# A decoder block: gate outputs in their own pool, column pairs alternating, rotation steps written later

## The chip, the cores and the metric

The kernel runs on one core of a Trainium2 chip. The metric is the device time of one execution in microseconds. TensorE (PE) multiplies, VectorE (DVE), ScalarE (ACT) and GpSimd (POOL) do the elementwise work, and all DMAs are issued from SyncE's queue (SP). An engine executes its own instructions in the order in which they stand in its queue, and a framework that turns the traced program into these queues decides that order from its own estimate of when each instruction is ready, unless the program pins it.

## The reference

A block of a decoder on 1024 tokens of width 1024, in float32. What matters here is the first half:

```
h = rms_norm(x, ln1_g)
proj = h @ w_in + b_in
rq, rk, rv, rg, aq, ak, av, gate_a, gate_b = split(proj)
rq, rk = rotary(rq), rotary(rk)             # 4 heads of 128
ry = head_group_norm(retention(rq, rk, rv)) # 4 heads of 256
branch_a = (silu(rg) * ry) @ w_ret_out
ay = sliding_window_sink_attention(rotary(aq), rotary(ak), av)
branch_b = ay @ w_attn_out
merged = sigmoid(gate_a) * branch_a + sigmoid(gate_b) * branch_b
x = x + merged @ w_out
x = x + (silu(h2 @ w_gate) * (h2 @ w_up)) @ w_down   # h2 = rms_norm(x, ln2_g)
return rms_norm(x, lnf_g)
```

## The kernel before

Every float32 operand of a matmul is split in a high and a low half, and a product is the sum of three matmuls (high by high, high by low, low by high). A split is a ScalarE copy (the high half) and a VectorE subtraction (the low half), lines 125 to 127. Stages follow each other on one PE queue:

- **Attention** (from 272). The pool `w1` holds all its tiles. While 32 units of attention run, PE's free time is filled with the 16 gate columns (`gate`, 470 to 476): each gate column is two halves of 24 matmuls in a PSUM bank of the tag `acc`, a tanh on ScalarE into a tile of the tag `st` (473), and a write of that tile to the DRAM tensor `tb_d` (475). After the last attention unit, `fl.rest()` (513) finishes the gates that are left. Then `w1` closes.
- **Retention values** (562 to 687). The pool `rvp` opens where `w1` was; it holds `vacc`, an accumulator of 32 KB a partition, whose free parts are scratch space first. The product `h @ w_rv` is done by a scheme of seven half-size products (P1 to P7, in the place of eight), each of four steps of 12 matmuls (line 646). Before the first step VectorE makes sums and differences of quarters of `h` in `vacc` (lines 660 to 676, 13 additions and subtractions of 128 x 1024, by `vadd` and `vsub`, lines 577 and 580), with the splits of the first two weight blocks (`vprep`, which writes `vP`) behind them. VectorE and ScalarE are pinned to the written order here (`in_order`, 659; the helper is at 101).
- **Column pairs** (690 to 815). The eight pairs of 128 columns for retention's k, q and swish gate are computed by the same scheme: `wseq` (698) lists the 56 products, 12 matmuls each (770), pair by pair with neighbours interleaved. `cols` (559) lists the pairs: four for k and q, then four for the gate. At each product, `wprep_to` splits the operand of the product two ahead; with the first two blocks of a pair it issues four weight differences on POOL (`gsub`, 516). `wproduct` issues the matmuls, keeps partial results (`p1`, `u2`, `u3`, line 775), and hands each of the four finished 128 x 512 results of a pair to `wresult` (735). For a gate pair that is an addition (755), a Silu (757) and a write to `rg_d` (758). For a k or q pair it is an eviction with the bias (743 or 745) into a tile `r`, two DMAs that swap the halves of its partitions into `xw` (747, 748), a multiplication of `r` by the cosines on VectorE (749), one of `xw` by the sines on POOL (750), their sum on VectorE (751), and a write to `rk_d` (752). The tables of cosines and sines sit in the buffers `kT` and `qT` of the pool `kq` (693), which head 0's k and q take over afterwards (`load_kq`, 799). P3 of a pair adds to the PSUM bank (`wB`) that P5 left, and can begin only when the result that reads that bank has been evicted. The order of VectorE, ScalarE and POOL is left to the framework in this stage.
- **Retention** (818 on). The pool `w2` opens over the places of the two previous pools; `load_v` (839) and `load_g` (845) fetch what the heads need, `k_transpose` turns k, and the output columns of attention (`bb_g`, 829), which read `ay` (loaded by `load_ay`, 792), fill PE's time. The first of `w2`'s instructions wait for the release of the pools below.

Then come the merge, the output product and the FFN, on which the diff does not touch.

Of the kernel before, what the change touches and what calls it, by code (L numbers as in the profile page):

```python
# [10 lines left out]
F32 = mybir.dt.float32  # L11
# [3 lines left out]
ALU = mybir.AluOpType  # L15

P = 128
# [9 lines left out]
RH = 4  # L27
AH = 16
C_RQ, C_RK, C_RV, C_RG, C_AQ, C_AK, C_AV, C_GA, C_GB = (
    0, 512, 1024, 2048, 3072, 4096, 4224, 4352, 5376)  # L30


def f32(t):
    return t.bitcast(F32)
# [3 lines left out]
def hybrid_block(ctx: ExitStack, tc: tile.TileContext, x, ln1_g, w_in, b_in, ret_norm_g, w_ret_out,  # L38
                 attn_sinks, w_attn_out, w_out, ln2_g, w_gate, w_up, w_down, lnf_g,
                 c_ident, c_atab, c_rtab, c_amask, c_rmask, c_rcol, out):  # L40
    nc = tc.nc
    x = x[0]
    out = out[0]
# [18 lines left out]
    rk_d = dram.tile([8, P, S], F32, name="rk_d")  # L62
# [37 lines left out]
    @contextmanager  # L100
    def in_order(*engines):

        traced = nc.cur_bb.bb.instructions
        last = traced[-1]
        yield
        start = next(k for k in reversed(range(len(traced))) if traced[k] is last) + 1
        prev = {}
        for i in traced[start:]:
            if i.engine in engines:
                if i.engine in prev:  # L110
                    tc.add_manual_dep(i, prev[i.engine],
                                      mybir.DependencyInfo(mybir.DependencyClass.NoSync, mybir.DependencyReason.DATA),
                                      reason="in_order")
                prev[i.engine] = i.name
# [41 lines left out]
    def dense_g(src, col, X, evac, name):  # L156
        w = slab(src, col, name)
        for half in range(2):
            pt = acc(f"acc_{name}_{half}")
            yield from mm_g(pt, w, X, half * 512)  # L160
            evac(half, pt)
            yield
# [57 lines left out]
    for t in range(NB):  # L220
# [3 lines left out]
        if 1 <= t <= 2:  # L224
            raw = raw_slab([8, P], f"kv{t}")
            c = C_AK if t == 1 else C_AV
# [42 lines left out]
    nc.vector.tensor_scalar(out=nsink, in0=nsink, scalar1=-1.0, scalar2=None, op0=ALU.mult)  # L269


    with tc.tile_pool(name="w1", bufs=1) as w1:
        atab = w1.tile([P, 2, S], F32, name="atab")
        nc.sync.dma_start(atab, c_atab.rearrange("z p s -> p z s"))
        amask = w1.tile([P, 256], F32, name="amask")
# [4 lines left out]
        def r512(tag, bufs, name):  # L280
            return w1.tile([P, 512], F32, tag=tag, bufs=bufs, name=name)
# [188 lines left out]
        def gate(n):  # L470

            def evac(half, pt):
                t = r512("st", 2, f"tb{n}{half}")
                nc.scalar.activation(t, pt, AF.Tanh, bias=bhalf[:, n:n + 1], scale=0.5)
                nc.sync.dma_start(tb_d[n, :, half * 512:half * 512 + 512], t)
            return dense_g(w_in, C_GA + n * P, H, evac, f"g{n}")
# [11 lines left out]
        for i in range(NU + 1):  # L488
# [7 lines left out]
            if i > 0:  # L496
                u_values(i - 1)
                if i % 4 == 0:
                    g, b, _, Bt, jb, _ = geo(i - 1)
                    c = slice((b // 4) * 512, (b // 4) * 512 + 512)  # L500
# [7 lines left out]
            if i == 3 * NB:  # L508

                for k in range(4):  # L510
                    nc.gpsimd.tensor_tensor(out=wv[:, 4 + k, :], in0=wv[:, 12 + k, :], in1=wv[:, 4 + k, :],
                                            op=ALU.subtract)
# [43 lines left out]
    def kq_pair(name, shape):  # L556
        return [kq.tile([P] + shape, F32, tag=t, name=f"{name}{t}") for t in ("kT", "qT")]

    cols = [C_RK, C_RQ, C_RK + 256, C_RQ + 256] + [C_RG + 256 * h for h in range(RH)]
    NW = len(cols)  # L560

    with tc.tile_pool(name="rvp", bufs=1) as rvp:
# [96 lines left out]
        with in_order(nc.vector.engine, nc.scalar.engine):  # L659
# [18 lines left out]
            for n in range(28):  # L678
                pr, k = VORDER[n // 4], n % 4
# [13 lines left out]
    rtab = kq_pair("rtab", [S])  # L693
    for z in range(2):
# [3 lines left out]
    wseq = [(0, "P2"), (1, "P2"), (0, "P1"), (1, "P1"), (0, "P6"), (0, "P5"), (0, "P7"), (1, "P6"), (0, "P4"), (0, "P3"),  # L698
            (1, "P5"), (1, "P7"), (2, "P1"), (1, "P4"), (1, "P3"), (2, "P2")]
# [7 lines left out]
    def wprep_to(n):  # L707
        while wready[0] < min(n, len(wseq)):
            j, pr = wseq[wready[0]]
            r0, r1 = wraw[j]  # L710
            b11, b12, b21, b22 = r0[:, :, 0:P], r0[:, :, P:2 * P], r1[:, :, 0:P], r1[:, :, P:2 * P]
            b = {"P1": b11, "P5": b11, "P7": b12, "P2": b21, "P4": b21, "P3": b22}.get(pr)
            if b is None:
                b = wtms[j]
            o = ring.tile([P, 2, 4, P], F32R, tag=("wh", "wl")[wready[0] % 2], name=f"w{j}{pr}")
            split(b, o[:, 0], o[:, 1])
            wops[j, pr] = o
            wdone.add((j, pr))
            if pr in ("P1", "P2") and {(j, "P1"), (j, "P2")} <= wdone:

                wtms[j] = wp.tile([P, 4, P], F32, tag="tt", bufs=2, name=f"wt2_{j}")
                gsub(b11, b12, b11)
                gsub(wtms[j], b22, b11)
                gsub(b12, b22, b12)
                gsub(b21, b21, wtms[j])
            if pr == "P3" and j + 2 < NW:
                wload_pair(j + 2)
            wready[0] += 1

    wbank, wkeep = {}, {}  # L730

    def wtile(tag, bufs, name):
        return wp.tile([P, 512], F32, tag=tag, bufs=bufs, name=name)

    def wresult(j, half, y, pt, other):

        ct = cols[j] // P + y
        bias = bcol[:, ct:ct + 1]
        c = slice(half * 512, half * 512 + 512)
        r = wtile("r", 4, f"r{j}{half}{y}")  # L740
        if j < 4:
            if other is None:
                nc.scalar.activation(r, pt, AF.Identity, bias=bias, scale=1.0)
            else:
                nc.vector.scalar_tensor_tensor(out=r, in0=pt, scalar=bias, in1=other, op0=ALU.add, op1=ALU.add)
            xw = wtile("xw", 2, f"xw{j}{half}{y}")
            nc.sync.dma_start(xw[0:64, :], r[64:128, :])
            nc.sync.dma_start(xw[64:128, :], r[0:64, :])
            nc.vector.tensor_tensor(out=r, in0=r, in1=rtab[0][:, c], op=ALU.mult)
            nc.gpsimd.tensor_tensor(out=xw, in0=xw, in1=rtab[1][:, c], op=ALU.mult)  # L750
            nc.vector.tensor_tensor(out=r, in0=r, in1=xw, op=ALU.add)
            nc.sync.dma_start(rk_d[ct, :, c], r)
            return
        if other is not None:
            nc.vector.tensor_tensor(out=r, in0=pt, in1=other, op=ALU.add)
            pt = r
        nc.scalar.activation(r, pt, AF.Silu, bias=bias, scale=1.0)
        nc.sync.dma_start(rg_d[ct - C_RG // P, :, c], r)

    def wproduct(j, pr):  # L760
        kind = {"P1": "A", "P6": "A", "P7": "A", "P4": "A", "P2": "C", "P5": "B", "P3": "B"}[pr]
        first = pr in ("P1", "P2", "P5")
        if first:
            tag, bufs = {"A": ("acc", 3), "B": ("s", 2), "C": ("t", 2)}[kind]
            wbank[j, kind] = ps(tag, bufs, f"w{kind}{j}")
        pt = wbank[j, kind]
        o = wops.pop((j, pr))
        for k, (xh, xl) in enumerate(HX[pr]):
            for z, (w, v) in enumerate(((0, xh), (0, xl), (1, xh))):
                nc.tensor.matmul(pt, o[:, w, k, :], v, start=(first and k + z == 0), stop=(k == 3 and z == 2),  # L770
                                 skip_group_check=not first)

        def keep(tag, bufs):
            e = wtile(tag, bufs, f"{tag}{j}")
            nc.scalar.copy(e, pt)
            wkeep[j, tag] = e
        if pr == "P1":
            keep("p1", 2)
        elif pr == "P6":
            keep("u2", 2)  # L780
        elif pr == "P7":
            keep("u3", 1)
        elif pr == "P4":
            wresult(j, 1, 0, pt, None)
        elif pr == "P3":
            wresult(j, 0, 1, pt, wkeep.pop((j, "u2")))
        if pr in ("P5", "P7") and (j, "u3") in wkeep and (j, "B") in wbank:
            wresult(j, 1, 1, wbank[j, "B"], wkeep.pop((j, "u3")))
        if pr in ("P1", "P2") and (j, "p1") in wkeep and (j, "C") in wbank:
            wresult(j, 0, 0, wbank[j, "C"], wkeep.pop((j, "p1")))  # L790

    def load_ay(z):
        AY.append(act.tile([P, 8, 1024], F32R, tag="B", name=f"ay{z}"))
        for g in range(2):
            nc.sync.dma_start(f32(AY[z][:, 4 * g:4 * g + 4, :]), ay_d[2 * z + g])
# [3 lines left out]
    def load_kq(h, z):  # L799

        t = (kTs, qTs)[z][h] = kq.tile([P, S], F32, tag=("kT", "qT")[z], name=f"r{z}{h}")
        nc.sync.dma_start(t, rk_d[4 - 4 * z + h])

    for i, (j, pr) in enumerate(wseq):
        wprep_to(i + 3)
        wproduct(j, pr)
        if (j, pr) == (2, "P1"):
            load_ay(0)
        elif (j, pr) == (NW - 2, "P6"):
            load_kq(0, 0)  # L810
            load_kq(0, 1)
        elif (j, pr) == (NW - 1, "P7"):
            load_ay(1)
    wpp.__exit__(None, None, None)
    wsc.__exit__(None, None, None)

# [327 lines left out]
    for nh in range(2):  # L1144
# [20 lines left out]
        for t in range(NB):  # L1165
# [12 lines left out]
            if nh == 1:  # L1178
# [3 lines left out]
                r = rstd_of(m2, 1, f"ln2_{t}")  # L1182
# [249 lines left out]
    for pi, pr in enumerate(ORDER):  # L1432
# [23 lines left out]
        for tt in range(4):  # L1456
            for f in range(cut, NP):
                mms(f, tt)
            half, z = {"P1": (0, 0), "P5": (1, 1), "P6": (0, 1), "P2": (0, 0), "P7": (1, 1), "P4": (1, 0),
                       "P3": (0, 1)}[pr]  # L1460
            t = 4 * half + tt
# [67 lines left out]
```

## Time and profile before

| what | value |
|---|---|
| median of 3 runs | 1643.65 us (1643.48 to 1647.53) |
| the profiled execution's own time | 1642.58 us |
| its span, first to last instruction | 1640.8 us |
| TensorE busy | 1585.0 us, 97% |
| VectorE busy | 971.6 us, 59% |
| ScalarE busy | 713.7 us, 43% |
| GpSimd busy | 384.4 us, 23% |
| mean granted TensorE clock | 0.987 |
| column pairs, first to last matmul | 498.4 to 661.9 us |

All times in the trace count from the span's start. A name such as `vacc` or `r` stands for all tiles of that name with numbers left out, `vacc<-h` means that `vacc` is written from `h`, and L646 is line 646. In the view of waits a line "A <- B: total, times, longest" tells how long the engine of A stood idle before that instruction because B was not done. In a timeline, brackets give the idle time before an instruction and what ended it. PEclk is the share of full speed that TensorE's clock was granted. SPq is SyncE's queue, where DMAs are issued.

### The profile page before, as it was taken

The numbers are of one execution on the slowest core, as the hardware profiler recorded it, in microseconds if no ns is written. First come the engines' busy times: TensorE is split into PE (matmuls) and PEld (weight loads), VectorE is DVE, ScalarE is ACT, GpSimd is POOL, SyncE is SP. The second block draws the span as 40 slices with busy tenths as digits, with TensorE's granted clock in tenths as the row PEclk, the third lists the DMA queues.
The fourth block names the chain that finished last, engine by engine and source line by source line (L and its number), as shares of the span: only waits on it lengthen the run. The fifth ranks groups of instructions, "written<-read, shape, count | busy, mean of one in ns | idle before, by whom it ended". The sixth has DMA issues, their size and how long they took to land.

```text
span 1640.8 us, 20874 instructions
## 1 busy us (share of the span) xinstructions
PE 1585.0 (97%) x7507; PEld 1317.1 (80%) x7507; DVE 971.6 (59%) x1730; ACT 713.7 (43%) x1415; POOL 384.4 (23%) x321
## 2 busy tenths in 40 slices
PE   9999999998799899999999998999999999999998
PEld 8887888886688778878888886888888888788886
DVE  6468767662875673677655248544444444588756
ACT  5358777762223234454322145333333333344445
POOL 2000001000005551000000025655555666300001
PEclk9999999999899999999999999999999999999999
DMA  6554638223026452855454300333333333773323
GB/s 205 161 161 139 190 130 248 97 84 133 15 81 227 144 171 96 292 176 174 138 190 134 128 22 15 121 96 114 98 103 97 109 110 109 264 261 91 97 97 122
DMA packets 150869, 223.13 MB, mean 136 GB/s; under 512 B 9131, under 2 KB 83693, under 8 KB 149230
## 3 DMA queue, kind: packets, MB, share of 16 engines
q1 hardware_dynamic: 150766, 221.80, 41.6%
q8 instruction: 59, 0.97, 0.2%
q14 instruction: 44, 0.36, 0.1%
HBM read 149.67 MB, written 67.37 MB: 132 GB/s over the span
## 4 chain that ended last, share of the span: by engine, by line
PE 82%; DVE 8%; DMA 3%; ACT 3%; issue 2%; POOL 2%; SPq 0%; POOLq 0%; DVEq 0%; ACTq 0%
PE fA L1225 14%; PE fB L1225 7%; PE dA L1443 6%; PE dxP L1443 5%; PE wA L770 4%; PE acc_g L143 3%; PE acc_g L144 3%; PE acc_g L145 3%; PE fC L1225 3%; PE va L646 3%; PE vP L646 2%; PE acc_ba L145 2%; PE acc_ba L144 2%; PE acc_ba L143 2%; PE wo L1173 2%
## 5 line engine op out<-in xcount | busy, mean ns | idle before, releaser
L1443 PE MATMUL dA<-dwP,daP 128*128 128x512 f32 x528 | 121.4, 390 | 1.9 <-DVE dwP L127 1.9
L1443 PEld LDWEIGHTS dA<-dwP,daP 128*128 128x128 f32 x528 | 98.8, 188 | 23.8 <-DVE dwP L127 3.4
L143 PE MATMUL acc_g<-h,wh_g 128*128 128x512 f32 x256 | 100.3, 392 | 0.0
L144 PE MATMUL acc_g<-h,wh_g 128*128 128x512 f32 x256 | 100.2, 391 | 0.0
L145 PE MATMUL acc_g<-h,wl_g 128*128 128x512 f32 x256 | 99.9, 390 | 0.0
L1443 PE MATMUL dxP<-dwP,daP 128*128 128x512 f32 x396 | 90.2, 389 | 0.0
L1443 PEld LDWEIGHTS dxP<-dwP,daP 128*128 128x128 f32 x396 | 74.3, 188 | 15.4
L412 POOL COPY sc<-nsink 128x4 f32<-128x4 f32 x32 | 7.9, 249 | 308.5 <-PE pT L445 248.0
L1283 POOL TENSOR_TENSOR xf<-xf 128x512 f32<-128x512 f32 x44 | 70.0, 1592 | 35.9 <-issue 30.3
L427 ACT ACTIVATE sc<-sc,nm 128x257 f32<-128x257 f32 (+1 forms) x128 | 62.4, 491 | 26.3 <-DVE nm L424 26.0
L1236 POOL TENSOR_TENSOR xf<-xf 128x512 f32<-128x512 f32 x33 | 49.6, 1502 | 45.3 <-DVE xf L1241 26.7
L1246 ACT COPY xf<-fA 128x512 f32<-128x512 f32 x44 | 25.8, 588 | 75.8 <-PE fA L1225 75.8
L424 DVE CUSTOM_DVE_ANT_0 sc<-s,amask,nsink 128x256 f32<-128x256 f32 (+1 forms) x128 | 53.1, 460 | 9.4 <-PE s L421 9.0
L145 PEld LDWEIGHTS acc_g<-h,wl_g 128*128 128x128 f32 x256 | 48.1, 188 | 9.7
L143 PEld LDWEIGHTS acc_g<-h,wh_g 128*128 128x128 f32 x256 | 48.1, 188 | 9.2
L144 PEld LDWEIGHTS acc_g<-h,wh_g 128*128 128x128 f32 x256 | 48.1, 188 | 9.1
L127 DVE TENSOR_TENSOR dwP<-wd,dwP 128x512 fp32r<-128x512 f32 x77 | 54.7, 712 | 0.0
L1388 POOL TENSOR_TENSOR rs_f<-tot,mhalf 128x1 f32<-128x1 f32 x8 | 7.9, 992 | 197.9 <-DVE tot L1385 197.9
L516 POOL TENSOR_TENSOR wr_f<-wr_f 128x512 f32<-128x512 f32 x22 | 33.8, 1540 | 78.9 <-DVE t_4P L127 9.5
L143 PE MATMUL acc_bb<-ay,wh_bb 128*128 128x512 f32 x128 | 51.1, 401 | 0.0
L516 POOL TENSOR_TENSOR wr_wp<-wr_wp 128x512 f32<-128x512 f32 x8 | 11.5, 1436 | 167.6 <-DMA ay<-ay_d 148.0
L143 PE MATMUL aq<-h,wh_aq 128*128 128x512 f32 x128 | 50.1, 392 | 0.6 <-ACT wh_aq L362 0.6
(763 smaller groups left out, 4416.4 us busy)
## 6 DMA issues: line engine op xcount, KB each, us to landing
act_d<-xf SPq DMA_DIRECT2D x77, 256.0 KB, 2.1
daP<-act_d SPq DMA_DIRECT2D x21, 512.0 KB, 3.7
q_d<-stg SPq DMA_DIRECT2D x8, 1024.0 KB, 4.6
wr_g<-in_w_in SPq DMA_DIRECT2D x16, 512.0 KB, 5.2
q<-q_d SPq DMA_DIRECT2D x32, 256.0 KB, 6.2
tb_d<-tb SPq DMA_DIRECT2D x32, 256.0 KB, 2.1
ay_d<-q SPq DMA_DIRECT2D x8, 1024.0 KB, 6.1
ay<-ay_d SPq DMA_DIRECT2D x4, 2048.0 KB
```

The costliest lines, as they stand in the source:

```text
L127: nc.vector.tensor_tensor(out=lo, in0=raw, in1=f32(hi), op=ALU.subtract)
L143: nc.tensor.matmul(pt, hi[:, k, :], xh, start=(k == 0), stop=False)
L144: nc.tensor.matmul(pt, hi[:, k, :], xl, start=False, stop=False)
L145: nc.tensor.matmul(pt, lo[:, k, :], xh, start=False, stop=(k == 7))
L424: nc.vector.tensor_tensor_reduce(out=sc[:, j, 0:nk], in0=pt[:, jj * 256:jj * 256 + nk], in1=mk, scale=1.0, scalar=nsink[:, 4 * g + j:4 * g ...
L427: nc.scalar.activation(sc[:, j, 0:nk + 1], sc[:, j, 0:nk + 1], AF.Exp, scale=-1.0, bias=nm[:, j:j + 1], accum_out=den[:, j:j + 1])
L646: nc.tensor.matmul(vbanks[pr][tt], x_[:, c], w[:, u, :], start=(fresh and k + z == 0), stop=(k == 3 and z == 2), skip_group_check=not fresh)
L770: nc.tensor.matmul(pt, o[:, w, k, :], v, start=(first and k + z == 0), stop=(k == 3 and z == 2), skip_group_check=not first)
L1225: nc.tensor.matmul(pt, o[:, w, k, :], v, start=(first and k + z == 0), stop=(k == 3 and z == 2), skip_group_check=not first)
L1236: nc.gpsimd.tensor_tensor(out=dst[q], in0=dst[q], in1=sg[q], op=ALU.mult)
L1283: nc.gpsimd.tensor_tensor(out=o, in0=a, in1=b, op=op)
L1443: nc.tensor.matmul(banks[tt], a[:, u, c], w[:, v, :], start=(fresh and f + z == 0), stop=(f == NP - 1 and z == 2), skip_group_check=not fresh)
```

## The change

Three things change. The two gate tiles of the tag `st` move from `w1` to a pool `gt` of their own, which is allocated from the other side of SBUF, where the pool `kq` opens later. The list `cols` alternates: a k or q pair, a gate pair, and so on. And of a rotated result, only the eviction and the two swapping DMAs are issued at once; the two multiplications (`turn`) are written down two products later, the sum and the write to DRAM (`total`) three products later. For that `r` is split in two tags (`rr`, four buffers, for rotated results; `r`, two buffers, for gate results), `xw` has four buffers instead of two, and VectorE, ScalarE and POOL are pinned to the written order for the whole stage. The loads of head 0's k and q are written at the last pair's P5 instead of the seventh pair's P6.

```diff
-    with tc.tile_pool(name="w1", bufs=1) as w1:
+    with tc.tile_pool(name="gt", bufs=1, side="right") as gt, tc.tile_pool(name="w1", bufs=1) as w1:
...
-                t = r512("st", 2, f"tb{n}{half}")
+                t = gt.tile([P, 512], F32, tag="st", bufs=2, name=f"tb{n}{half}")
...
-    cols = [C_RK, C_RQ, C_RK + 256, C_RQ + 256] + [C_RG + 256 * h for h in range(RH)]
+    cols = [c for h in range(RH) for c in ((C_RK, C_RQ, C_RK + 256, C_RQ + 256)[h], C_RG + 256 * h)]
...
+    wlater, wnow = [], [0]
...
-        r = wtile("r", 4, f"r{j}{half}{y}")
-        if j < 4:
+        r = wtile(*(("r", 2) if j % 2 else ("rr", 4)), f"r{j}{half}{y}")
+        if j % 2 == 0:
...
-            xw = wtile("xw", 2, f"xw{j}{half}{y}")
+            xw = wtile("xw", 4, f"xw{j}{half}{y}")
             nc.sync.dma_start(xw[0:64, :], r[64:128, :])
             nc.sync.dma_start(xw[64:128, :], r[0:64, :])
-            nc.vector.tensor_tensor(out=r, in0=r, in1=rtab[0][:, c], op=ALU.mult)
-            nc.gpsimd.tensor_tensor(out=xw, in0=xw, in1=rtab[1][:, c], op=ALU.mult)
-            nc.vector.tensor_tensor(out=r, in0=r, in1=xw, op=ALU.add)
-            nc.sync.dma_start(rk_d[ct, :, c], r)
+
+            def turn():
+                nc.gpsimd.tensor_tensor(out=xw, in0=xw, in1=rtab[1][:, c], op=ALU.mult)
+                nc.vector.tensor_tensor(out=r, in0=r, in1=rtab[0][:, c], op=ALU.mult)
+
+            def total():
+                nc.vector.tensor_tensor(out=r, in0=r, in1=xw, op=ALU.add)
+                nc.sync.dma_start(rk_d[ct, :, c], r)
+            wlater.extend([(wnow[0] + 2, turn), (wnow[0] + 3, total)])
             return
...
-    for i, (j, pr) in enumerate(wseq):
-        wprep_to(i + 3)
-        wproduct(j, pr)
-        if (j, pr) == (2, "P1"):
-            load_ay(0)
-        elif (j, pr) == (NW - 2, "P6"):
-            load_kq(0, 0)
-            load_kq(0, 1)
-        elif (j, pr) == (NW - 1, "P7"):
-            load_ay(1)
+    with in_order(nc.vector.engine, nc.scalar.engine, nc.gpsimd.engine):
+        for i, (j, pr) in enumerate(wseq):
+            wprep_to(i + 3)
+            wnow[0] = i
+            wproduct(j, pr)
+            while wlater and wlater[0][0] <= i:
+                wlater.pop(0)[1]()
+            if (j, pr) == (2, "P1"):
+                load_ay(0)
+            elif (j, pr) == (NW - 1, "P5"):
+                load_kq(0, 0)
+                load_kq(0, 1)
+            if (j, pr) == (NW - 1, "P7"):
+                load_ay(1)
+        assert not wlater
```

## Prediction, made before the result was known

> **What bounds the kernel now.** I read the page first: spans, the busy shares, the chain that ended last.
>
> ```profile
> span 1640.8 us, 20874 instructions
> ...
> PE 1585.0 (97%) x7507; PEld 1317.1 (80%) x7507; DVE 971.6 (59%) x1730; ACT 713.7 (43%) x1415; POOL 384.4 (23%) x321
> ...
> PE 82%; DVE 8%; DMA 3%; ACT 3%; issue 2%; POOL 2%; SPq 0%; POOLq 0%; DVEq 0%; ACTq 0%
> ```
>
> TensorE (PE) bounds it. Its 56 us without a matmul are all that a change of waits can win, so the next question is in which stages they lie. The table of busy time by stage answers that (us, then busy time of each engine with its instructions, granted clock, DMA share, GB/s).
>
> ```profile
> core 0: us, PE busy (x) PEld busy (x) DVE busy (x) ACT busy (x) POOL busy (x), PEclk, DMA share, GB/s
> ...
> 400.70:433.10 32.40, 13.70 (x50) 10.62 (x49) 27.90 (x27) 5.51 (x8) 0.00 (x0) 0.68 0.18 57
> ...
> 498.40:529.00 30.60, 30.60 (x136) 25.34 (x136) 17.59 (x23) 10.37 (x18) 16.99 (x13) 1.00 0.68 227
> 529.00:605.00 76.00, 68.45 (x288) 54.52 (x288) 54.31 (x60) 23.10 (x39) 43.78 (x28) 0.98 0.49 146
> 605.00:661.90 56.90, 56.90 (x252) 46.73 (x252) 20.51 (x29) 26.66 (x43) 12.18 (x9) 1.00 0.42 144
> ```
>
> Two holes lie where the diff works: the start of the retention value product (400.7 to 433.1) and the rotated column pairs (529 to 605). The gate columns behind them (605 to 661.9) leave PE no hole. The chain gives each stage's ends and the pace of PE, and the waits name who is late.
>
> ```profile
> 401.86 1.99 DMA tb_d<-tb
> 404.33 2.37 DVE vacc L577 x2
> ...
> 420.70 12.40 PE va L646 x44
> 433.10 10.88 PE vP L646 x48
> ...
> 498.38 5.44 PE wC L770 x24
> ...
> 659.15 2.72 PE wB L770 x12
> ```
> ```profile
> DVE vacc L577 <- DMA tb_d<-tb: 23.1, 1, 23.1
> ...
> PE va L646 <- DVE vP L127: 18.3, 1, 18.3
> ```
>
> Twelve matmuls take 2.72 us where nothing is late (48 take 10.88). At 401.86 the last gate tile leaves for DRAM; only when it has landed does VectorE (DVE) begin its sums, and PE waits for the weight split that stands behind them.
>
> **The first hole: 21.1 us to win.** The value product is 28 steps of 12 matmuls, 28 x 2.72 = 76.2 us, and takes from 400.7 to 498.38, 97.7 us: 21.5 lost. What holds DVE is not the data:
>
> ```profile
> 375.76 0.43 DVE L468 TENSOR_TENSOR q<-tm,q 128x256 fp32r<-128x256 f32 x1 [0.47 <-ACT q L467]
> 379.96 1.23 DVE L127 TENSOR_TENSOR wl_g<-wr_g,wh_g 128x1024 fp32r<-128x1024 f32 x1 [3.77 <-ACT wh_g L126]
> ...
> 419.96 1.29 DVE L127 TENSOR_TENSOR vP<-wv,vP 128x512 fp32r<-128x512 f32 x2
> ```
> ```profile
> 401.89 0.50 PE L646 MATMUL va<-vP,h 128*128 128x512 f32 x1 [0.39 <-ACT tb L474]
> ```
>
> The sums read h, which has long been there; vacc lies in rvp, whose place was w1's. In the built program vacc (bytes 184064 to 216832 of a partition) does not touch the two gate buffers (225152 to 229248), and still waits for them: a new pool waits for all of the pool that it overlaps. With the gate tiles in gt, at the other side of SBUF, w1 is done with attention's last tiles, read at 375.76. DVE is then free from 381.2 (379.96 + 1.23). From 404.33 to the end of the first split at 420.6 it needs 16.3 us, so it would be ready at 397.5, 3.2 us ahead of the last gate matmul at 400.7. That gate work is the cover; without it the 16.3 come back. What is late next is a PSUM bank, which the last tanh frees: the 0.39 us in the last row stay, hence 21.1. kq now inherits gt's place and its wait for the landing at 403.9; its first tile is written after the second step of P1, past 406, so nobody waits. The third split needs a ring slot that the last gate gives back at its end, 400.7; its step comes two steps later, at 406.1.
>
> Of the 21.5, 2.4 are not waiting but slow matmuls: 44 should take 10.0 us and took 12.40, and the clock shows it.
>
> ```profile
> 420.66:425.00 4.34, 4.30 (x10) 3.43 (x11) 4.27 (x5) 0.48 (x1) 0.00 (x0) 0.50 0.02 4
> ```
>
> The granted clock is 0.50 for the first 4.3 us behind the wait, so removing the wait removes this as well. The Trainium skill (TensorE: Matmul & The Clock Gate, "What's actually happening") has an idle array at half clock until about 3.4 us of work release it, which would price this at 1.7 us as an estimate, and the first hole at 20.4; the 0.50 agrees, the length in this trace is longer.
>
> **The second hole: 11.2 us, of which I take 9.7.** 56 products x 2.72 = 152.3 us; from 498.38 to 661.87 they take 163.5, so 11.2 are lost. One rotated result, then the totals over the stage:
>
> ```profile
> 536.89 0.76 DVE r L745
> ...
> 538.23 4.31 DMA xw<-r
> ...
> 542.69 1.82 POOL xw L750
> ...
> 544.54 0.70 DVE r L751
> ```
> ```profile
> PEld wB L770 <- DVE r L745: 6.4, 3, 2.5
> ```
> ```profile
> DVE r L749 <- DMA xw<-r: 15.9, 9, 3.8
> ...
> DVE r L751 <- POOL xw L750: 11.1, 10, 2.4
> ```
>
> A result is evicted (536.89 + 0.76), its halves are swapped by two DMAs, GpSimd (POOL) multiplies, DVE adds. DVE works in order: its 27 us of waiting for the DMA and for POOL hold the next eviction, and P3 may not write bank B before that eviction has read it. The swap has landed 4.9 us after the eviction (537.65 to 542.54), POOL ends at 6.9. The change issues the multiplications two products later (5.44 us) and the add three later (8.16): 0.5 and 1.3 us to spare. The moved instructions are unchanged in number: per rotated result one POOL and two DVE operations, two swap DMAs and one write of rk_d; the swaps stay at the eviction, and the write goes down SP's queue behind the next result's swaps instead of ahead of them. Four xw and four rr buffers cover three products in flight. Alternation spreads the load: DVE's 92.4 us in the stage and POOL's 73.0 (three rows above) are 61% and 48% of 152.3, where now the rotated stretch has 71% and 58%. Pinning POOL puts a result's multiplication behind the four weight differences of the next pair, and DVE's add behind that. Not shown before; bounds: 0, as the gate columns lose, and 11.2, as now. I take 1.5, near the lower, because two products' slack (5.44) lies between an eviction and the matmul that needs its bank. A gain below 0 is excluded, PE being full there.
>
> The functions now alternate on ScalarE too (Identity, Silu). The trace has one load for it:
>
> ```profile
> 589.98 1.28 ACT L757 ACT_TABLE_LOAD   x1
> ```
>
> No second one appears when Identity returns at L945, so Silu's table serves both: one load, now at the first gate pair, with ScalarE at 30 to 47% busy (rows above): nothing. ScalarE is pinned as well: the copy for product i + 2 stands ahead of the eviction of product i, but its slot came free with product i - 2, so it holds nothing up.
>
> **The end of the stage: 1.5 us given back.** The last rotated pair is now last but one.
>
> ```profile
> 597.50 0.43 SPq L802 DMA_DIRECT2D r<-rk_d  x1
> ...
> 654.50 0.80 SPq L795 DMA_DIRECT2D ay<-ay_d  x2
> 658.98 4.73 SPq L758 DMA_DIRECT2D rg_d<-r  x3
> ...
> 670.98 0.59 SPq L843 DMA_DIRECT2D rv<-v_d  x1
> ```
> ```profile
> 679.32 0.36 PE L879 MATMUL u<-vh,kt 128*128 128x256 f32 x1 [0.25 <-issue]
> ```
> ```profile
> 660.00:670.00 10.00, 10.00 (x50) 8.38 (x49) 1.82 (x2) 1.54 (x2) 0.00 (x0) 1.00 1.00 364
> ```
> ```profile
> ACT kt L859 <- DMA rg_d<-r: 7.3, 1, 7.3
> ```
> ```profile
> DMA to landing us min/median/max: 7.1/7.1/7.1
> ```
>
> Loading head 0's k and q must wait for the cos and sin tables in the same buffers, now free four products (10.9 us, less POOL's 1.8) before the stage's end instead of 64.4 us before it. These 1.05 MB come close to the 4.2 MB of ay, in a stretch where the DMA engines are full: 0 to 2.9 us (1.05 MB at 364 GB/s). SP has them written behind ay, but it issues what its schedule finds ready (the present load, written at the seventh pair, went at 597.5), and the tables come free a little before P7 frees ay's place, which is three products or 8.2 us before the end. Gate results have two buffers instead of four: the last add must wait for the write issued at 658.98; at the last write's 7.1 us (last row) it lands at 666.1, against the add's 661.9: 0 to 4.2 us, in which DVE's split for the second output column waits too. All of w2 waits for the last landing, then come v's load and the matmul at 679.32, which has no slack. Bounds 0 and 7.1; I take 1.5, since fewer bytes are left to fetch by then.
>
> **Sum.** The profiled execution took 1642.58 us, 1.8 around its span and 1.07 below the median of 1643.65. 1642.6 - 21.1 - 11.2 + 1.5 + 1.5 = 1613.3; on the median's footing 1614.4.
>
> **Rivals.**
> (a) The first wait stays, because the release of gt still counts for rvp. For: vacc already waits without touching the tiles. Against: gt lies outside rvp. 1643.65 - 9.7 + 1.5 = 1635.5; chance 0.06.
> (b) The port that DVE and POOL share. A DVE operation of 0.70 us (the add above) took 1.77 while POOL subtracted:
>
> ```profile
> 555.99 1.77 DVE L749 TENSOR_TENSOR r<-r,rtabkT 128x512 f32<-128x512 f32 x1
> ```
> ```profile
> 555.48 1.74 POOL L516 TENSOR_TENSOR wr_wp<-wp,wr_wp 128x512 f32<-128x512 f32 x1
> ```
>
> Each turn now issues POOL's multiplication just ahead of DVE's own, so 16 x 1.07 = 17.1 us may be added to DVE. On PE's path in full it replaces the 11.2: 1643.65 - 21.1 - 11.2 + 17.1 + 1.5 = 1630.0; if it only keeps the hole as it is, 1624. Against: DVE's 39% idle. The Trainium skill (SBUF — State Buffer, "Who interferes with whom") says that the operation issued second fully blocks, which speaks against writing these two together; the 1.77 agrees. Chance 0.08.
> (c) The end of the stage costs its upper bound: 1614.4 + 5.6 = 1620. Chance 0.12.
> (d) Slower: the pinned DVE stands at every rotated result. If swaps land later than two products, say 7.0 us, the longest that POOL waited for one, each of 16 results costs 7.0 - 5.44 = 1.6 for the landing and 1.82 for POOL behind it: 54.7 us, 1643.65 - 32.3 + 54.7 = 1666. It turns the sign above 2.0 us per result. Against: 4.31 in a stretch of mean DMA share 0.49. Chance 0.02.
>
> ```profile
> POOL xw L750 <- DMA xw<-r: 29.0, 10, 7.0
> ```
>
> **Numbers.** The forecast has 0.72. The range, 1611 (nothing given back) to 1626, takes in (c) and the lower part of (b). About 0.3%, 4.9 us, is what a measurement of this kernel can tell from no change. Forecast, (a), (b) and (c) are faster by more: 0.96 with some left for mixtures; 0.02 within; 0.02 slower.
>
> **What would show it.** Right: DVE's first vacc sum at about 381, PE's first va step without a wait of over 1 us and a clock of 1.00 there; the 56 products in 152 to 155 us; PE waiting for L745 nowhere; xw's multiplication waiting under 1 us. Wrong: vacc waiting for tb_d, a clock below 1.00 in the column stage, PE idle at the first u by more than 3 us, or a stage that grew elsewhere.

## The result and the profile after

The changed kernel takes 1617.99 us (median of 4 runs, 1615.2 to 1620.9). Beside it on the same chip the kernel before took 1643.48 to 1647.53 us in three runs; a fourth took 4109.04 us and is left out of the ratio. The ratio is 0.9837 (95% interval 0.9808 to 0.9866). The profiled execution took 1616.76 us. Forecast were 1614.4 us, 1611 to 1626: faster, as said, and 3.6 us above the number.

The page of the changed kernel, the lines that answer to the first three of the prediction:

```profile
span 1615.0 us, 20843 instructions
...
PE 1579.4 (98%) x7507; PEld 1315.3 (81%) x7507; DVE 976.0 (60%) x1730; ACT 712.0 (44%) x1415; POOL 380.5 (24%) x321
...
PE 84%; DVE 6%; ACT 3%; DMA 3%; issue 2%; POOL 1%; SPq 0%; POOLq 0%; ACTq 0%; DVEq 0%
```

The span is 25.8 us shorter, DVE's share of the chain is down from 8 to 6%. To see where the time came from, one needs marks that both kernels have. Two are good: the first transposition of k (`kTT`), which PE reaches right behind the last of the 56 products, and the first matmul of the output product `acc_ba`, which ends the retention heads. Their instructions, kernel before and kernel after (the last two times are the first and the last start):

```profile
L770 PE MATMUL wC<-h,w0P x12: 389/389/389, 498.2 to 500.7; 128*128 128x512 f32 x12
L856 PE MATMUL kTT<-ident,r x32: 270/272/273, 661.7 to 765.0; 128*128 128x128 f32 x32
L143 PE MATMUL acc_ba<-yg,wh_ba x128: 389/389/477, 808.6 to 895.1; 128*128 128x512 f32 x128
```

```profile
L777 PE MATMUL wC<-h,w0P x12: 389/389/389, 477.3 to 479.8; 128*128 128x512 f32 x12
L868 PE MATMUL kTT<-ident,r x32: 270/272/273, 630.3 to 739.5; 128*128 128x128 f32 x32
L143 PE MATMUL acc_ba<-yg,wh_ba x128: 389/389/476, 783.4 to 869.9; 128*128 128x512 f32 x128
```

| stretch | before | after | difference | forecast |
|---|---|---|---|---|
| up to the first of the 56 products | 498.2 | 477.3 | -20.9 | -21.1 |
| the 56 products | 163.5 | 153.0 | -10.5 | -9.7 (-11.2 + 1.5) |
| from there to `acc_ba` | 146.9 | 153.1 | +6.2 | +1.5 |
| the rest | 832.2 | 831.6 | -0.6 | 0 |

The two holes closed as forecast. The third row is the miss: the heads behind the stage lose 6.2 us, not 1.5. First the holes. The chain of the changed kernel, with the start, the length and the work of each piece, and then the table of busy time by stage:

```profile
401.21 10.93 PE va L646 x48
412.14 10.88 PE vP L646 x48
...
466.55 10.88 PE va L646 x48
477.43 5.44 PE wC L777 x24
```

```profile
core 0: us, PE busy (x) PEld busy (x) DVE busy (x) ACT busy (x) POOL busy (x), PEclk, DMA share, GB/s
400.70:433.10 32.40, 32.40 (x145) 26.73 (x144) 24.12 (x31) 14.27 (x20) 0.00 (x0) 1.00 0.09 34
477.30:630.30 153.00, 152.84 (x673) 125.78 (x672) 95.75 (x111) 57.26 (x98) 68.66 (x48) 1.00 0.53 166
...
655.00:660.00 5.00, 4.53 (x26) 4.26 (x25) 3.77 (x12) 2.38 (x6) 0.00 (x0) 0.69 0.45 145
```

The value product now begins at once, 48 matmuls in 10.9 us, and the clock stays at 1.00 where it was 0.68 on average; in the 56 products PE is busy for 152.84 of 153.00 us. DVE had its sums done ahead of it, as its timeline shows:

```profile
376.15 0.43 DVE L468 TENSOR_TENSOR q<-tm,q 128x256 fp32r<-128x256 f32 x1 [0.47 <-ACT q L467]
376.66 2.36 DVE L577 TENSOR_TENSOR vacc<-h 128x1024 f32<-128x1024 f32 x2
...
393.31 1.28 DVE L127 TENSOR_TENSOR vP<-wv,vP 128x512 fp32r<-128x512 f32 x2
...
397.03 1.23 DVE L580 TENSOR_TENSOR vacc<-vacc 128x1024 f32<-128x1024 f32 x1
```

The first sum stands right behind attention's last tile; nothing waits for `tb_d`. Now the third row. SyncE's timeline, then DVE's, around the end of the 56 products, the waits there, and a line of ScalarE's timeline:

```profile
618.95 0.32 SPq L809 DMA_DIRECT2D r<-rk_d  x1
...
623.03 0.85 SPq L802 DMA_DIRECT2D ay<-ay_d  x2
628.12 0.90 SPq L765 DMA_DIRECT2D rg_d<-r  x2
629.07 6.66 SPq L132 DMA_DIRECT2D wr_bb<-in_w_attn_out  x2
640.18 0.34 SPq L765 DMA_DIRECT2D rg_d<-r  x1
...
643.48 0.45 SPq L853 DMA_DIRECT2D rmask<-in_c_rmask  x1
643.97 0.59 SPq L855 DMA_DIRECT2D rv<-v_d  x1
```

```profile
626.65 0.69 DVE L762 TENSOR_TENSOR r<-wB,u 128x512 f32<-128x512 f32 x1
638.71 0.69 DVE L762 TENSOR_TENSOR r<-wB,u 128x512 f32<-128x512 f32 x1 [11.37 <-DMA rg_d<-r]
641.67 1.23 DVE L127 TENSOR_TENSOR wl_bb<-wr_bb,wh_bb 128x1024 fp32r<-128x1024 f32 x1 [2.28 <-ACT wh_bb L126]
```

```profile
POOL xw L753 <- DMA xw<-r: 45.0, 12, 8.7
...
DVE r L762 <- DMA rg_d<-r: 11.4, 1, 11.4
...
PE u L891 <- issue: 3.6, 1, 3.6
```

```profile
652.85 1.34 ACT L912 ACTIVATE vh<-rv,rcol 128x512 fp32r<-128x512 f32 x2 [4.73 <-DMA rv<-v_d]
```

Read them in this order. The last gate addition stands still for 11.4 us, until 638.71, since of the two buffers neither is free: the write that would free one was issued at 628.12 and took 10.6 us. Its own result is written at 640.18 (at about 632 where it has not to wait, as in e3 below). The pool `w2` opens behind that write, and the mask's and v's loads go out at 643.5 and 644.0, 3.3 and 3.4 us later than in e3. The first `u` comes at 653.7, 23.4 us behind the first `kTT` (before: 679.3 - 661.7 = 17.6). The view of waits names nothing for which PE stands still there ("issue"), but `u` reads `vh`, and ScalarE makes `vh` only at 652.85, when v has landed. PE is idle for 3.6 us in front of `u`, and its granted clock is 0.69 from 655 to 660.

### The profile page after: what moved, and what is told of

Its sections match the earlier page's. It is cut to its first block, busy times and chain, and to the rows that moved or that the text cites. A ratio compares the mean times of both kernels' runs of the same rounds, so it can differ in the third digit from the quotient of the medians.

```text
span 1615.0 us, 20843 instructions
## 1 busy us (share of the span) xinstructions
PE 1579.4 (98%) x7507; PEld 1315.3 (81%) x7507; DVE 976.0 (60%) x1730; ACT 712.0 (44%) x1415; POOL 380.5 (24%) x321
## 4 chain that ended last, share of the span: by engine, by line
PE 84%; DVE 6%; ACT 3%; DMA 3%; issue 2%; POOL 1%; SPq 0%; POOLq 0%; ACTq 0%; DVEq 0%
PE fA L1237 14%; PE fB L1237 7%; PE dA L1455 6%; PE dxP L1455 5%; PE wA L777 5%; PE acc_g L143 4%; PE acc_g L144 4%; PE acc_g L145 4%; PE fC L1237 3%; PE va L646 3%; PE wB L777 2%; PE vP L646 2%; PE acc_ba L143 2%; PE acc_ba L144 2%; PE acc_ba L145 2%; PE wo L1185 2%
## 5 line engine op out<-in xcount | busy, mean ns | idle before, releaser
L1258 ACT COPY xf<-fA 128x512 f32<-128x512 f32 x44 | 25.8, 588 | 76.1 <-PE fA L1237 76.1
L126 ACT CAST daP<-daP 128x512 fp32r<-128x512 f32 x42 | 26.1, 622 | 56.2 <-PE dxP L1455 26.7
```

## The experiments

Four runs share a chip with each other and with the kernel before, three times: the kernel before took 1644.06 us there beside the first four, 1644.47 beside the next and 1643.87 beside the last (medians). Times from the traces: "products" is the first of the 56 to `kTT`, "u" and "acc_ba" are counted from `kTT`.

| run | what | median us | ratio to before, 95% | products | u | acc_ba |
|---|---|---|---|---|---|---|
| e1_gt_only | pool `gt` alone | 1622.07 | 0.9871 (0.9856 to 0.9885) | 162.5 | 18.1 | 146.9 |
| e2_no_gt | all but `gt` | 1637.71 | 0.9964 (0.9951 to 0.9977) | 153.0 | 23.0 | 151.9 |
| e3_r3 | three gate buffers | 1610.67 | 0.9802 (0.9786 to 0.9818) | 153.0 | 18.5 | 145.8 |
| e4_old_cols | e3, old column order | 1610.76 | 0.9802 (0.9788 to 0.9817) | 153.0 | 18.0 | 145.6 |
| e5_alt_only | e3, steps at once, no pin | 1612.42 | 0.9806 (0.9789 to 0.9822) | 152.6 | 18.7 | 148.0 |
| e6_no_pin | e3, no pin | 1610.99 | 0.9799 (0.9784 to 0.9814) | 152.6 | 19.6 | 150.4 |
| e7_actq | gate writes from ScalarE's queue | 1615.94 | 0.9829 (0.9815 to 0.9844) | 152.9 | 22.4 | 152.9 |
| e8_r3_actq | e3 and e7 | 1617.10 | 0.9835 (0.9820 to 0.9850) | 152.9 | 22.7 | 153.5 |
| e9_again | the change once more | 1615.63 | 0.9829 (0.9814 to 0.9844) | 153.0 | 23.7 | 155.7 |
| e10_r3_again | e3 once more | 1610.38 | 0.9792 (0.9777 to 0.9806) | 153.0 | 18.8 | 147.5 |
| e11_ay_late | half of `ay` behind the gate writes | 1607.85 | 0.9781 (0.9768 to 0.9794) | 153.0 | 19.1 | 144.2 |
| e12_r3_ay_late | e3 and e11 | 1608.65 | 0.9787 (0.9774 to 0.9800) | 153.0 | 16.6 | 144.6 |

**Each part alone.** Only the pool, on the kernel before; and all the rest without it.

```diff
-                t = r512("st", 2, f"tb{n}{half}")
+                t = gt.tile([P, 512], F32, tag="st", bufs=2, name=f"tb{n}{half}")
```

> The kernel before with the gate tiles in the pool gt and nothing else. If the first hole is the release of w1 alone, the value product starts at about 401 without a wait, the 56 products of the column pairs keep their 163 us, the stage's end keeps its order, and the time is 21 us under before: about 1623.5. If the closing of gt with w1 still held it, 1644.

> The changed kernel with the gate tiles back in w1. The value product waits again (DVE's first sum at about 404, 21 us lost); the column pairs take 153 us instead of 163.5, and the first u comes about 6 us later after the last product than before. If the two parts simply add, 1644.5 - 10.5 + 6.2 = about 1640.

The pool alone gains 22.0 us, the rest alone 6.4, together 28.3; the whole change gains 28.2 on the third chip (1643.87 - 1615.63). So the parts add up and do not meet. Without the pool, VectorE waits as in the kernel before:

```profile
DVE vacc L577 <- DMA tb_d<-tb: 23.1, 1, 23.1
```

Without the rest, the products take 162.5 us, and the heads behind them run as before (18.1, 146.9; before: 17.6, 146.9). What is given back at the end therefore belongs to the column stage's part, not to `gt`, nor to the earlier start of everything.

**Which of the two terms of the end.** The theory: two gate buffers, by a write that lands late. The rival: head 0's 1.05 MB, which now lie close to `ay`.

```diff
-        r = wtile(*(("r", 2) if j % 2 else ("rr", 4)), f"r{j}{half}{y}")
+        r = wtile(*(("r", 3) if j % 2 else ("rr", 4)), f"r{j}{half}{y}")
```

> The changed kernel with three buffers for gate results instead of two. Theory A (two buffers): the last gate addition no longer waits for a write to land (11.4 us now), the last write lands 8.6 to 10 us after the last product instead of about 12, the first u comes 17.4 to 19 us after it instead of 23.2, and the time falls by 4 to 6 us to about 1613. Theory B (bytes): head 0's k and q, now fetched just ahead of ay, push everything behind them; the addition doesn't wait, but the last landing and u stay as late as now, and the time stays at 1618.

With a third buffer the loads of k and q lie where they did, and all of the 6.2 us are gone (145.8 against 146.9 before). The last addition in the timeline of VectorE waits for its bank alone, and `w2`'s loads go out 3 us earlier:

```profile
630.56 0.69 DVE L762 TENSOR_TENSOR r<-wB,u 128x512 f32<-128x512 f32 x1 [3.19 <-PE wB L777]
```

```profile
628.15 4.25 SPq L765 DMA_DIRECT2D rg_d<-r  x3
...
640.15 0.34 SPq L853 DMA_DIRECT2D rmask<-in_c_rmask  x1
```

One thing besides the wait differs. With the other buffer count the framework puts 48 matmuls of the attention output between the first `kTT` and `rs`, where the changed kernel has 60 (the kernel before 45), and keeps some to fill in behind `u`. So the gain is that of the edit with the order that comes with it.

The two kernels were then run on one chip, five rounds each:

> The changed kernel once more, nothing altered, beside the version with three gate-result buffers on one chip. Theory (two buffers cost 6 to 7 us at the stage's end): 1616 to 1619 us, 5 us or more above the three-buffer version. Rival (the 7 us between them were in part a difference of the chips or days): under 4 us above it.

> The changed kernel with three gate-result buffers once more, nothing else altered. Theory: 1609.5 to 1612 us, 5 us or more below the changed kernel on the same chip. Rival: 1612 to 1615 us.

The difference stands, 1615.63 against 1610.38 us, 5.3 us, and the intervals of the ratios do not touch. Between traces of one kernel the last column of the table moves by 2 to 3 us (153.1 and 155.7 for the change, 145.8 and 147.5 with three buffers), so the medians are the better measure of what is lost.

**Why the write lands late.** It stands behind `ay` in SyncE's queue. Either the queue keeps it waiting, or the bytes do, in whichever queue it stands. The first edit takes it to another queue, the second halves what is ahead of it (`load_ay_rest` issues the other 2.1 MB behind the last gate write, held there by a dependency).

```diff
-        nc.sync.dma_start(rg_d[ct - C_RG // P, :, c], r)
+        nc.scalar.dma_start(rg_d[ct - C_RG // P, :, c], r)
```

> The changed kernel with its two gate-result buffers; only the writes of the gate results to DRAM are issued from ScalarE's queue instead of SyncE's, where ay's 4.2 MB stand ahead of them. Theory (the write that the last gate addition waits for lands late because it stands behind ay in the same queue): the wait of 11.4 us falls below 4 us, the first u comes 18 to 19 us after the last product, 1610 to 1613 us. Rival (the 16 DMA engines are full whatever queue the write comes from): the wait stays at 8 us or more and the time at 1616 to 1619 us.

```diff
-        for g in range(2):
+        for g in range(2 - z):
             nc.sync.dma_start(f32(AY[z][:, 4 * g:4 * g + 4, :]), ay_d[2 * z + g])
...
         assert not wlater
+        load_ay_rest()
```

> The changed kernel with its two gate-result buffers; of ay's last 4.2 MB the second half is issued only behind the last gate write, so that the write that the last gate addition waits for has 2.1 MB less ahead of it on SyncE's queue. Theory (bytes ahead of the write set its landing): at 364 GB/s 2.1 MB are 5.8 us, the wait of 11.4 us becomes 5 to 6, the first u comes 18 to 20 us after the last product, 1610.5 to 1614 us, unless the output product has to wait for the half that comes late. Rival (it waits for it: issued at about 632.5 it lands at about 638.5 or later, and the product needs it near 635): TensorE waits 3 us or more for ay in the output product, and the time is 1616 to 1621 us.

The timelines of e7 (VectorE, and ScalarE's queue) and of e11 (VectorE, and SyncE's queue):

```profile
627.42 0.33 ACTq L765 DMA_DIRECT2D rg_d<-r  x1
...
629.82 1.22 DVE L127 TENSOR_TENSOR wl_bb<-wr_bb,wh_bb 128x1024 fp32r<-128x1024 f32 x1 [3.28 <-ACT r L764]
637.87 0.69 DVE L762 TENSOR_TENSOR r<-wB,u 128x512 f32<-128x512 f32 x1 [6.83 <-DMA rg_d<-r]
```

```profile
622.12 0.32 SPq L802 DMA_DIRECT2D ay<-ay_d  x1
627.21 0.90 SPq L765 DMA_DIRECT2D rg_d<-r  x2
...
631.52 0.69 DVE L762 TENSOR_TENSOR r<-wB,u 128x512 f32<-128x512 f32 x1 [5.10 <-DMA rg_d<-r]
...
636.97 0.33 SPq L861 DMA_DIRECT2D rmask<-in_c_rmask  x1
```

The wait in e7 is shorter on paper, 6.8 us, only because a weight split was put ahead of the addition. What counts is when the addition can begin: 637.87, 8.3 us behind that run's `kTT` at 629.6. In the changed kernel it is 638.71 - 630.3 = 8.4. Another queue brings nothing; the theory that the write would come early in a queue of its own falls. With 2.1 MB less ahead the addition begins 631.52 - 629.4 = 2.1 us behind `kTT`, 6.3 us earlier; 2.1 MB at the 364 GB/s of the prediction's row are 5.8 us. It is the bytes of `ay`. They hold the write in a different way in each queue, as the view of the DMAs shows (packets, MB, share of the 16 engines; q1 is SyncE's queue, q10 ScalarE's). The changed kernel from 628.12 to 635, and e7 from 632 to 636:

```profile
DMA packets 178, 2.65 MB, mean 386 GB/s; under 512 B 16, under 2 KB 16, under 8 KB 16
```

```profile
q1 hardware_dynamic: 92, 1.51, 88.2%
q10 hardware_dynamic: 89, 0.17, 11.4%
```

On SyncE's queue the write stands behind `ay`: up to 635 only packets of 16 KB move besides 16 tiny ones, while a gate write is made of packets of 2 KB. On ScalarE's queue its packets move in turn with those of `ay`, about one for one, but each of `ay`'s carries eight times as much. A gate write has 144 packets (2304 for all 16), and by 636 ScalarE's queue has moved 126 since the write was issued. So in both kernels the write is done only when `ay` nearly is, and that the two figures are as close as 8.3 and 8.4 is in part luck. The Trainium skill (DMA: Bandwidth & Descriptors, "Issuing engines are not separate DMA queues") has transfers from all issuing engines run on the same 16 DMA engines; the shares of q1 and q10, 88.2 and 11.4%, agree. Another section of that page ("Queues, rings and completion order") lets each DMA engine serve its queues in turn, packet by packet; the 92 and 89 packets agree.

The feared wait of TensorE for the late half of `ay` did not come: `ay` is in none of e11's waits of PE. At 1607.85 us e11 is the fastest of all, 7.8 us below the change on the same chip, with two gate buffers as in the change. How much of the 2.5 us to e10 is the early write is open, since the framework also reordered matmuls of the attention output there.

**Two combinations.**

> Three gate-result buffers and, besides, the writes of the gate results issued from ScalarE's queue. If what is left of the stage's end (first u 18.5 us after the last product) is set by the landing of the last gate write behind ay, which opens w2's pool, the mask's load is issued under 7 us after the last product instead of 9.7, and the time is 1606 to 1609 us. Rival (v's load stands behind ay anyway, and the end is set by ay's bytes): 1609.5 to 1612 us, as with three buffers alone.

> Three gate-result buffers and the second half of ay's last 4.2 MB behind the last gate write. If the landing of the last gate write is what opens w2's pool (mask's load 9.7 us after the last product), that load comes 4 us or more earlier, and the time is 1607 to 1610 us. Rival (TensorE waits for ay's late half instead): 1612 to 1616 us.

e8 is a miss for both its theories. The third buffer frees the addition (629.77), but the mask's load still goes out 10.6 us behind `kTT` (640.18 - 629.6), not under 7, and the time is that of e7. In both runs the framework, given other queues, put the retention product `rs` earlier in PE's queue, ahead of matmuls of the attention output that stand before it in the changed kernel. PE waits for it, in e8 and then in e7:

```profile
PE rs L900 <- DVE kt L872: 6.1, 1, 6.1
```

```profile
PE rs L900 <- DVE kt L872: 6.7, 1, 6.7
```

So e7's and e8's totals judge that order too, and only the start of the addition was used above. e12 came out as its first theory had it: the mask's load goes out 5.3 us behind `kTT` (e3: 9.8), and the time lies between 1607 and 1610. But it is no better than e11 (the intervals overlap). The mask's load (7.6 in e11) and `u` come over 2 us earlier than there, and the heads end no earlier (144.6 against 144.2); what limits them then is open.

**What closes the second hole.** The change has three means for it: the distance of two and three products, the alternation, the pin. They were taken out of e3, the pin once alone and once with the distance. The four `xw` buffers, two before, stayed in all of these runs, and e4 has head 0's loads at their old place as well:

```diff
-    cols = [c for h in range(RH) for c in ((C_RK, C_RQ, C_RK + 256, C_RQ + 256)[h], C_RG + 256 * h)]
+    cols = [C_RK, C_RQ, C_RK + 256, C_RQ + 256] + [C_RG + 256 * h for h in range(RH)]
```

> The changed kernel with the columns in the old order (four rotated pairs, then four gate pairs), three buffers for gate results, and head 0's loads at the old place. Theory C (lag): writing the steps two and three products later closes the second hole by itself; the 56 products take 152 to 154 us and the time is 1612 to 1614, since the end of the stage is as before. Theory D (spreading): with VectorE 71% and GpSimd 58% busy in the rotated stretch the lag is not enough; the products take 157 to 163 us, and the time is 1617 to 1623.

```diff
-            wlater.extend([(wnow[0] + 2, turn), (wnow[0] + 3, total)])
+            turn()
+            total()
...
-    with in_order(nc.vector.engine, nc.scalar.engine, nc.gpsimd.engine):
+    if True:
```

> The changed kernel with three gate-result buffers, but a rotated result's two multiplications and its add are written down at once, as before the change, and no engine is pinned; the alternation of the columns stays. Theory C (it is the distance of two and three products that closes the second hole, the alternation does nothing for it): DVE waits again for the swap and for GpSimd, about 4.9 and 1.9 us for each of 16 results, and the 56 products take 159 to 164 us instead of 152.9; 1616 to 1622 us. Theory D (spreading the rotated columns is enough by itself, as a gate column's products lie between two rotated results and give DVE time): 152.9 to 155 us for the products and 1610.5 to 1613 us.

> The changed kernel with three gate-result buffers, without pinning VectorE, ScalarE and GpSimd to the written order in the column stage; the distance of two and three products is still written down. Theory: a written distance is kept only where the order is pinned, the scheduler otherwise moves the steps forward to where it takes them for ready, DVE waits for swaps again, and the products take 155 us or more: 1613 to 1620 us. Rival (the pin is not needed, the written order is what the scheduler works from): no wait, 152.9 us for the products, 1609.5 to 1612 us.

The waits of VectorE in the products, e4 (distance and pin without alternation) and then e5 (alternation without distance and pin):

```profile
DVE r L754 <- DMA xw<-r: 2.0, 3, 0.9
DVE r L757 <- POOL xw L753: 0.5, 1, 0.5
```

```profile
DVE r L757 <- POOL xw L753: 8.9, 7, 2.4
DVE r L754 <- DMA xw<-r: 7.3, 7, 1.7
```

The distance takes most of the waits away; the alternation leaves 16 us of the 27, and they no longer reach PE. Why they do not is argued, not shown: a gate pair's products lie between those of two rotated pairs. Either closes the hole (153.0 and 152.6 us), and neither closes more of it in company. No run has the old two `xw` buffers, so their part is open.

My theory for e5, that only the distance does it, fell; so did the one for e6: without the pin VectorE waits again (3.7 and 13.2 us in that run), and the products still take 152.6. Both runs end the heads 2 to 5 us later than e3 in the trace, but the medians, on other chips, do not tell them from it by more than the intervals. I leave open whether the distance or the pin is worth a microsecond there.

SyncE's queue also made swaps late in the kernel before:

```profile
SPq L752 <- DVE r L751: 44.9, 14, 6.0
```

SyncE stands 44.9 us in front of the writes of rotated results, waiting for their sums, and swaps of the next result stand behind such a write: the first half of one is issued at 538.97, its second half at 545.62, right behind the write at 545.26. Written three products later, the writes hold SyncE for 11.9 us. In e5 they hold it for 46.4 again, and the products still take 152.6, so this alone did not make the hole.

## Why the prediction was right, and where it was not

- **First hole, 21.1 us: right.** 20.9 measured; e1 has 20.0 of it by the trace with nothing else changed. That `vacc` waited for the tiles of a tag because they lay in the pool `w1` is shown: the tag's move undoes the wait (e1), and e2 brings it back. The half clock went with the wait: the granted clock is 1.00 there. One detail was off: DVE's first sum came at 376.7, not 381, because the gate split that I had ahead of it (379.96) came later than the first sums. It changed nothing: PE had no wait for it at either.
- **Second hole, 11.2 with 1.5 kept: right, and a little better.** 10.5 measured, 0.7 kept of the 163.5 - 152.3. But the reason was too narrow: I put the gain down to two products' slack, and e5, which has the alternation and not the slack, closes the hole as well. Of the signs that I named, PE waits for line 747 (745 before) nowhere, while "xw's multiplication waiting under 1 us" was badly chosen and failed: POOL waits 45.0 us for the swap, and neither VectorE nor PE waits for POOL's product. The sign that means something is VectorE's wait for swap and product, 27.0 us before, which is gone from the list.
- **Rival (b), the shared port: not in the changed kernel.** VectorE's 16 multiplications with the cosines take 14.2 us in all (886 ns each, 14.0 before), the 16 additions 13.3 (17.0 before). The distance is not the reason, or not alone: in e4, which has it with the pin, the multiplications take 19.9 us, in e5 18.4, in e6 19.7. Of the variants, only those with distance, alternation and pin together keep them at 14. And where VectorE lost up to 5.7 us so, the products took 152.6 to 153.0 us all the same. So a part of the feared 17.1 us exists, but not on PE's path.
- **End of the stage, 1.5 given back: this step failed; 6.2 were.** The place and the cause were named in the prediction: "the last add must wait for the write issued at 658.98". The size was wrong, by 4.7 us; with 0.2 less won in the first hole, 0.8 more in the second and 0.6 in the rest of the kernel this is the 3.5 us by which the sum misses in the trace. The term had two parts, with an upper bound of 7.1 for both, and I chose near the bottom, "since fewer bytes are left to fetch by then". The buffers' part was priced too low: I let the write land after 7.1 us, the time of a later write, which had less of `ay` ahead of it (the last of the three), and bounded the addition's delay by 4.2. The write took 10.6, and the addition began at 638.71 where three buffers let it begin at 630.56, 8.1 later. When the write was issued at 628.12, some 3.05 MB of `ay` had still to move (186 packets of 16 KB); at the 369 GB/s from there to 638.71 that is 8.3 us, and 2.0 us is the shortest landing of a gate write in the kernel before: 10.3 of the 10.6. The bytes' part, bounded by 2.9, was small: of k's and q's loads and the writes beside them 1.04 MB had moved between 618.95 and 623.03, before `ay` was issued, and about 0.7 MB moved among the first packets of `ay`. Halving `ay` in front of it (e11) moved it by the bytes' worth, and a third buffer (e3) made it harmless. With three buffers the old order of columns and loads (e4) changes the heads' end by 0.2 us and brings the mask's load 0.7 us nearer (9.1 against 9.8 us behind `kTT`), so k's and q's bytes cost next to nothing by themselves. Whether two buffers with the old loads would have got by was not tried. Rival (c), the upper bound of this term at 1620 us, came nearer than the forecast; it had a chance of 0.12.
- **Rivals (a) and (d):** e2 shows what (a) would have looked like (1637.71 us; priced at 1635.5), and no rotated result held the pinned VectorE.

## What to carry to other kernels

When a buffer's release hangs on a small write, sum the bytes that are still to move when it is issued, divide by the rate at which the DMA engines are full, and add the landing of a write that has nothing ahead of it: here 8.3 + 2.0 us for 10.6. A queue of its own did not help here, since the two queues took turns by packets and the write's were small. A term with a wide range wants an argument for the value taken in it; the one given here spoke for one of its two parts. And where several means are put in against one stall, take them out in turn: here the distance with the pin and the alternation each did without the other, while the two buffers for gate results, four before, made the loss at the end.

## What the runs showed of the hardware

- A gate write, 128 x 512 of float32, issued on SyncE's queue with 3.05 MB of a load in front of it, frees its buffer after 10.6 us; the shortest landing of such a write was 2.0 us.
- Issued on ScalarE's queue, it frees its buffer no earlier (8.3 against 8.4 us behind the last product). The two queues moved 92 and 89 packets in 4 us, of 16 and 2 KB, so the queue with the small packets got 0.17 of 1.68 MB.
- VectorE's multiplication of 128 x 512, both inputs in SBUF, took 886 ns on average in the changed kernel and 1148 to 1244 ns in e4 to e6, where the same instructions of VectorE and GpSimd stand in another order.
- Behind a wait of PE of 3.6 us in front of `u` the granted clock was 0.69 from 655 to 660, in a stretch where e3, which waits 0.2 us, has 1.00.
